# A hybrid attention, mLSTM and Hyena backbone: score, filter-tap and decay products on all 128 rows of the matrix array

## The chip, the cores and the metric

The kernel runs on one core of a Trainium2 chip. The metric is device time in microseconds (us) of one execution, the median of several runs.

## The reference

The program is a two-layer backbone over 512 latent tokens and 256 context tokens of width 1024. What matters here are three small pieces of each layer.

```python
# windowed attention: 8 query heads, 2 key groups, head width 64, blocks of 128 queries
s_loc = einsum('bntkgd,bnskd->bnkgts', qb, kb) * scale      # the block and its neighbours, masked
s_ctx = einsum('bntkgd,bckd->bnkgtc', qb, kc) * scale       # 256 context keys
p = softmax(concatenate([s_sink, s_ctx, s_loc]))
...
# Hyena filter taps: 64 features of every position times w3
h = jnp.sin(freq[1] * (h @ w2 + b2))
h = (h @ w3).reshape(L, HY_ORDER, 2, HY_WIDTH)
...
# mLSTM within a chunk of 128 tokens
dmat = where(tril, b[..., :, None] - b[..., None, :] + ic[..., None, :], -inf)
mt = maximum(a, max(dmat, -1))
s = einsum('bhtd,bhsd->bhts', qc, kc) * exp(dmat - mt[..., None])
```

The rest of a layer is an adaLN-modulated norm, one wide input projection, a gated merge of the three mixers, an output projection and a convolutional FFN.

## The kernel before

Channels lie on the partitions and tokens in the columns. A value that needs full precision is kept as two float32r tiles, a high part and a low part, and a product of two such values is three matrix products: high by high, low by high, high by low. The large products (`kstep`, line 401) run like that with 128 by 128 weights and up to 512 columns; their weights come from memory as 512 KB tiles and are split on ScalarE (line 339) and VectorE (line 340).

The work of the mixers is written as Python generators. Each is a "lane", and `tick` lets lanes emit some of their instructions after each step of the large products, at rates written in `RATE`. So TensorE's queue is one static order in which mixer products are strewn between large products, and an operation that waits holds all that are behind it. Tiles come from pools: `T` tiles are 768 columns wide, `H` tiles 512, with counts by stage in `SIZES`; a new tile waits until one of its kind is free.

Three places use only half of the array's 128 rows.

- **Scores.** Heads are 64 wide, so `stacked` (line 792) lays a query's 64 high rows and 64 low rows over the 128 partitions. A key's high rows stand there twice (two copies by DMA from the POOL queue, lines 801 and 802), so one product on 128 rows gives (q high + q low) by k high (line 1037). The key's low parts stand once, in one tile: group 0 on rows 0 to 63, group 1 on rows 64 to 127. Line 1038 multiplies them with the query's high rows alone, on 64 rows, into the same columns. An item of `att_mix` is a block of 128 queries, a pair of heads and a key group. A latent item has four such pairs of products (two heads, context keys and local keys) and masks added by bfloat16 products (line 1049); a context item has two pairs. Layer 0 has 16 latent and 8 context items, layer 1 has 16 latent ones. The scores go to one PSUM tile with a single buffer, which the maxima (VectorE, line 1063) and exponentials (ScalarE, line 1067) read before the next item's scores may be written. Then come `normalize`, transposes (line 1093), their copies into `H` tiles named pT (lines 1103 and 1105) and the products with the values (line 1119), whose outputs take 64 columns of the array.
- **Filter taps.** `filter_taps` multiplies 64 features with w3. `hd` holds their high rows over their low rows; `w3h` and `w3l` hold the weights' parts, which came twice, on all 128 rows. Line 654 takes all rows of `hd` and `w3h`, line 655 the upper 64 rows of `hd` and `w3l`. There are four sets of 4 products for the 512 tokens in each layer and four sets of 2 for the context in layer 0: 40 in all.
- **Decays.** `ml_gates` leaves the running maxima as two tensors of 64 rows (high and low parts) in memory, and `ml_load` reads them into two tiles of 64 rows from the POOL queue. In `prep`, for each of 4 heads, 2 directions and each group of up to four chunks, two products on 64 rows (line 1351) with a column of a negated identity (`nident`, 64 rows, line 281) spread the row of one head over all partitions, first the high parts and then the low ones, and a bfloat16 product adds the mask (line 1353). Layer 0 has groups of 512 and of 256 columns, layer 1 only groups of 512: 24 groups.

The stages of a layer are: A (gates, with norms, modulation and filters beside them), the attention's projections (`att_proj`, then `att_finish`), the attention beside the mLSTM's projections, the mLSTM beside the Hyena projections, E (Hyena and merges), and the FFN, in which layer 0 also runs layer 1's filters.

Of the kernel before, what the change touches and what calls it, by code (L numbers as in the profile page):

```python
# [32 lines left out]
# order of the m-tiles of the stacked [D_MODEL, 128] weights of a layer  # L33
# [12 lines left out]
# columns of the packed per-channel vectors of a layer  # L46
# [11 lines left out]
# ---------------------------------------------------------------- constants of the shapes  # L58
# [70 lines left out]
# ---------------------------------------------------------------- layout of the inputs  # L129
# [82 lines left out]
# ---------------------------------------------------------------- the program  # L212
class Two:
    """latent and context columns in two tiles"""
# [24 lines left out]
class Prog:  # L239
# [3 lines left out]
    SIZES = {'A0': (18, 26), 'A1': (8, 41), 'mix': (20, 21), 'E': (16, 29), 'ffn0': (20, 23), 'ffn1': (30, 0)}  # L243
# [17 lines left out]
    def __init__(self, tc, es, aps, dbg=None):  # L261
        self.tc, self.nc, self.a, self.dbg = tc, tc.nc, aps, dbg or {}
        nc = self.nc
        self.n = 0
        self.lanes, self.deferred, self.late = [], [], []
        pool = lambda name, bufs, **k: es.enter_context(tc.tile_pool(name=name, bufs=bufs, **k))
        self.cp = pool("const", 1)
        self.wp = pool("weights", 2)
        self.hp = pool("hl", 16)
        self.dp = pool("dram", 1, space=DRAM)  # L270
        self.pg = pool("psg", 3, space=PSUM)
        c = self.cp
        a = aps
        self.cv = c.tile([P, 16], F32, name="cv")
        nc.sync.dma_start(self.cv, a["cv"])
        self.ident = c.tile([P, P], F32, name="ident")
        make_identity(nc, self.ident)
        self.identb = c.tile([P, P], BF16, name="identb")
        nc.vector.tensor_copy(self.identb, self.ident)
        self.nident = c.tile([64, 64], F32R, name="nident")  # L280
        nc.vector.tensor_scalar(self.nident, self.ident[:64, :64], -1.0, None, op0=ALU.mult)
        self.ones = c.tile([P, P], F32, name="ones")
        nc.vector.memset(self.ones, 1.0)
        self.eps = c.tile([P, 1], F32, name="eps")
        nc.vector.memset(self.eps, EPS)
        self.sv = [c.tile([P, NSV], F32, name=f"sv{l}") for l in range(DEPTH)]
        self.fg = c.tile([P, KD], F32, name="fg")
        self.rope = c.tile([P, 2, SEQ], F32, name="rope")
        self.maskb = c.tile([P, 2, P], BF16, name="maskb")
        self.mod = [c.tile([P, 48, 2], F32, name=f"mod{l}") for l in range(DEPTH)]  # L290
        self.A = {(l, i): c.tile([P, KD, 2], F32, name=f"A{l}{i}") for l in range(DEPTH) for i in (1, 2)}
        self.sil = c.tile([P, KD, 32], F32, name="sil")
        self.g_dram = {}
# [8 lines left out]
    # ---- small helpers  # L302
# [39 lines left out]
    # ---- weaving of the mixers' work into the stream of matrix products  # L342
# [26 lines left out]
    def fill(self, n):  # L369
        """work put by for the places where the products have to wait"""  # L370
        for _ in range(n):
            next(self.spare, None)
# [11 lines left out]
    # ---- GEMM  # L384
# [34 lines left out]
    def proj_first(self, l, ms, parts):  # L419
        """three m-tiles, part by part, two of them k outermost: the operands may still be coming"""  # L420
        ws = [self.weight(self.a["wA"][l, m]) for m in ms]
        joint = parts[-1][1] <= 512
        if joint:
            one = [self.G() for _ in ms]
        outs = [[] for _ in ms]
        for i, (lo, hi, _) in enumerate(parts):
            if i:
                self.run_deferred()
            pss = [ps[:, lo:hi] for ps in one] if joint else [self.G() if i == 0 else self.M() for _ in ms]
            for group in ((0, 1), (2,)) if i == 0 else ((0,), (1,), (2,)):  # L430
                for k in range(KD):
                    for j in group:
                        self.kstep(pss[j], ws[j], slice(k * P, k * P + P), self.hlh[k], self.hll[k], lo, hi, k == 0, k == KD - 1)
                    self.tick(3 * len(group) * max(0.109, (hi - lo) * 0.422e-3))
            for o, ps in zip(outs, pss):
                o.append((lo, hi, ps))
        self.run_deferred()
        return [[(0, parts[-1][1], ps)] for ps in one] if joint else outs
# [12 lines left out]
    def fine_parts(self, l):  # L451
        """parts that the end of one product and the start of the next go through one after the other"""
        return self.parts(l) if l < DEPTH - 1 else [(0, 256, 0), (256, SEQ, 0)]

    # ---- adaLN modulation
# [9 lines left out]
    def ada(self, l, blocks):  # L465
        """blocks of 512 of the six vectors; the groups of k-tiles side by side in the array's columns"""
# [25 lines left out]
    # ---- norms  # L492
# [56 lines left out]
    # ---- Hyena filters in the frequency domain  # L549
# [20 lines left out]
    def filters(self, l, L, resident, overlap):  # L570
        """spectra of the filters, by order and half of the channels: filter taps, then their DFT"""
# [17 lines left out]
        # [high; low] parts of the 64 features, which came twice  # L589
# [27 lines left out]
    def filter_taps(self, l, L, hd, dec, it, out):  # L617
# [21 lines left out]
        for t in range(nT + 1):  # L639
# [12 lines left out]
            if t < nT:  # L652
                ps = self.M()
                nc.tensor.matmul(ps, hd[:, t * P:(t + 1) * P], w3h, start=True, stop=False)
                nc.tensor.matmul(ps, hd[0:64, t * P:(t + 1) * P], w3l[0:64], start=False, stop=True)
# [23 lines left out]
    def filter_dft(self, l, L, gc, it, sd):  # L679
# [9 lines left out]
        def dft(c, half):  # L689
            """cos / -sin, high and low parts, [tau tile][k] of a half of the taps"""  # L690
# [40 lines left out]
    # ---- projections  # L731
# [4 lines left out]
    def conv(self, l, dst, outs, w, b):  # L736
        """width-3 depthwise convolution of the tokens, the latent and the context ones apart"""
# [40 lines left out]
    def rope_swap(self, q):  # L778
        """the halves of each head's channels in each other's place"""
# [12 lines left out]
    def stacked(self, x, n, key):  # L792
        """per kv group the parts of 64 channels over all the partitions:
        a query's high part (at its group's place) and its low part; a key's high part twice, and apart its low part"""
        nc = self.nc
        top, bot, low = self.T("x0", dt=F32R), self.T("x1", dt=F32R), self.T("xl", dt=F32R)
        for h, t in ((0, top), (64, bot)):
            nc.scalar.copy(t[h:h + 64, :n], x[h:h + 64, :n])
            nc.vector.tensor_tensor(low[h:h + 64, :n], x[h:h + 64, :n], t[h:h + 64, :n].bitcast(F32), op=ALU.subtract)
        if key:  # L800
            nc.gpsimd.dma_start(top[64:128, :n], top[0:64, :n])
            nc.gpsimd.dma_start(bot[0:64, :n], bot[64:128, :n])
            return top, bot, low
# [7 lines left out]
    def tok_major(self, src, dst):  # L811
        """the six chunks of columns of src, transposed, into a tile [P, 6, P] or into six tiles"""
# [21 lines left out]
    def fold(self, kind, half, base, L):  # L834
        """tiles of a half of the channels (kind 0: v, 1: x1), folded about the centre of the tokens"""
# [12 lines left out]
    def fold_tok(self, fs, H, jt):  # L848
        """one token tile of the folded channels, token-major [sum | difference]"""
# [7 lines left out]
    def pair_products(self, ps, g, sub, parts):  # L857
        """complex products of [real | imaginary] columns, each half split into its parts on its own"""
# [28 lines left out]
    def hy_mix(self, l, out):  # L887
        """the halves of the channels one after the other, the next one's start within the second order of the one before;
        the short sequence's halves side by side"""
# [122 lines left out]
    # ---- attention  # L1012
    def att_mix(self, l, out):
        """software pipeline over (block of queries, pair of heads, kv group)"""
# [11 lines left out]
        def scores(it):  # L1026
            qb, p, kv = it
            ds_ = slice(kv * 64, kv * 64 + 64)
# [3 lines left out]
            # head 0: the local keys end and its context keys begin at 512; head 1: context keys, then local keys from 1024  # L1032
            kh, kl = k[kv], k[2]

            def dots(o, j, ks, n, stop):
                qh = q[2 * p + j][kv]
                nc.tensor.matmul(ps[:, o:o + n], qh[:, self.chunk(qb)], kh[:, ks], start=True, stop=False)
                nc.tensor.matmul(ps[:, o:o + n], qh[ds_, self.chunk(qb)], kl[ds_, ks], start=False, stop=stop)
# [43 lines left out]
        def transposes(it, i0):  # L1082
# [6 lines left out]
            for i in range(n):  # L1089
                for j in range(2):  # L1090
                    # columns of the block in the row of head j
# [69 lines left out]
    # ---- mLSTM  # L1161
# [35 lines left out]
    def rev_copy(self, f, dst, src):  # L1197
        """[64, 768] rows: forward rows as they are, backward rows turned within the latent and the context part"""
# [19 lines left out]
    def ml_gates(self, l):  # L1218
# [3 lines left out]
        # log sigmoid(f) = min(f, 0) - ln(1 + exp(-|f|))  # L1222
# [51 lines left out]
        # natural token order  # L1274
# [33 lines left out]
    def ml_load(self):  # L1308
# [5 lines left out]
        self.ml["mn"] = [self.T("mn", [64, NT], F32R) for _ in range(2)]  # L1314
        for x in range(2):
            nc.gpsimd.dma_start(self.ml["mn"][x], self.mld[0:64, 2 + x, :])
# [4 lines left out]
    def ml_mix(self, l, out):  # L1321
# [9 lines left out]
        def prep(h):  # L1331
# [12 lines left out]
            for d in range(2):  # L1344
                r = d * 32 + h
                dt = self.T("dt", [P, 6, P])
                for i in range(0, nch, 4):
                    w = min(4, nch - i)
                    pt = self.M()
                    for x in range(2):  # L1350
                        nc.tensor.matmul(pt[:, :w * P], self.nident[:, r:r + 1].to_broadcast([64, P]),
                                         mn[x][:, i * P:(i + w) * P], start=(x == 0), stop=False)
# [9 lines left out]
        def chain(h):  # L1362
# [75 lines left out]
            # channel-major  # L1438
# [57 lines left out]
    def merge(self, l, r, branches, gates, y, b, nxt=None):  # L1496
        """y (+)= 2 sigmoid(gate_r) * (branch_r @ w_branch_r); after the last branch half of y, in high and low parts"""
# [47 lines left out]
    def ffn(self, l, x, part_done):  # L1545
# [6 lines left out]
        def down(c, last, ms=range(KD)):  # L1552
# [14 lines left out]
            if last:  # L1567
                # part by part; the weights stay if there is room for them, or come again
# [17 lines left out]
        for c in range(len(bounds) - 1):  # L1586
            for i in range(bounds[c], bounds[c + 1]):
# [16 lines left out]
                # some of the last but one product is left for the wait for the last one's operands  # L1604
# [165 lines left out]
```

## Time and profile before

| | us |
|---|---|
| median of 3 runs | 2808.58 (2805.72 to 2810.65) |
| span of the profiled execution | 2804.0 |
| TensorE busy | 2695.0 (96%) |
| VectorE busy | 1752.1 (62%) |
| ScalarE busy | 1051.3 (37%) |
| GpSimd busy | 282.1 (10%) |

The profiled execution's own time is not listed apart: its span is 4.6 us under the median. In the rows below, PE is TensorE's matmul, PEld its weight load, DVE VectorE, ACT ScalarE, POOL GpSimd and SP SyncE. "128*64 ... 128x256" is a matmul on 128 rows and 64 columns of the array with a 128 by 256 moving operand. A matmul's printed duration reaches from its start to the modelled end of its results, and the next one begins before that; how long it holds the array is read from one start to the next.

### The profile page before, as it was taken

To read this page: it belongs to the slowest core of one execution; us is meant where nothing else is said; L and a number is where in the kernel's file an instruction comes from. 1 tells how busy PE (TensorE), PEld (TensorE's weight loads), DVE (VectorE), ACT (ScalarE), POOL (GpSimd) and SP (SyncE) were. 2 spreads that over 40 slices of the span, in tenths; PEclk is the share of its full clock that TensorE was granted. 3 is DMA by queue.
4 is the path that set the end of the run, shared out by engine and by line. 5 is a ranking of instruction groups with operands and counts; after the bars stand their busy time and mean duration, and the time that the engine had idled before them with its cause. 6 is when DMAs were issued, how large, how long until landed. Compare 5 with 4: busy or idle time off the path is not lost. (4 is left out here: it accounts for less than half of the span.)

```text
span 2804.0 us, 38203 instructions
## 1 busy us (share of the span) xinstructions
PE 2695.0 (96%) x14762; PEld 2199.1 (78%) x14762; DVE 1752.1 (62%) x3076; ACT 1051.3 (37%) x1893; POOL 282.1 (10%) x297
## 2 busy tenths in 40 slices
PE   6899999999999998999999999999999999999998
PEld 2678787778888886787888887777787778888887
DVE  5685554556457765767667566655447477665666
ACT  4344343445323233433233234534345233533333
POOL 3241110000000301011101000210000002000000
PEclk8999999999999999999999999999999999999999
DMA  7555331122436542354443224541222556333332
GB/s 257 168 199 195 108 95 38 38 66 91 151 130 207 174 155 70 116 169 143 132 131 91 68 65 149 185 136 40 76 91 94 185 183 211 98 98 98 97 95 65
DMA packets 153158, 347.66 MB, mean 124 GB/s; under 512 B 15553, under 2 KB 52910, under 8 KB 152976
## 3 DMA queue, kind: packets, MB, share of 16 engines
q1 hardware_dynamic: 132976, 319.03, 34.3%
q0 software_dynamic: 20000, 26.19, 3.7%
q8 instruction: 117, 1.92, 0.3%
q14 instruction: 65, 0.53, 0.1%
HBM read 287.02 MB, written 52.17 MB: 121 GB/s over the span
## 5 line engine op out<-in xcount | busy, mean ns | idle before, releaser
L401 PE MATMUL pg<-hh,wh 128*128 128x512 f32 (+1 forms) x2536 | 923.8, 365 | 7.9 <-ACT hh L339 6.2
L401 PE MATMUL pg<-hlo,wh 128*128 128x512 f32 (+1 forms) x2536 | 900.7, 355 | 4.1 <-DVE hlo L340 3.9
L401 PE MATMUL pg<-hh,wl 128*128 128x512 f32 (+1 forms) x2536 | 898.6, 355 | 0.1
L340 DVE TENSOR_TENSOR wl<-wr,wh 128x1024 fp32r<-128x1024 f32 x294 | 370.3, 1260 | 304.1 <-ACT wh L339 296.2
L401 PEld LDWEIGHTS pg<-hh,wh 128*128 128x128 f32 x2536 | 483.4, 191 | 94.5 <-issue 26.7
L401 PEld LDWEIGHTS pg<-hlo,wh 128*128 128x128 f32 x2536 | 484.3, 191 | 67.2 <-DVE hlo L340 6.8
L401 PEld LDWEIGHTS pg<-hh,wl 128*128 128x128 f32 x2536 | 483.1, 191 | 66.2 <-issue 1.5
L339 ACT CAST wh<-wr 128x1024 fp32r<-128x1024 f32 x294 | 308.8, 1050 | 567.2 <-PE pg L401 525.3
L1527 DVE SCALAR_TENSOR_TENSOR x<-pg,mod,x 128x512 f32<-128x512 f32 (+1 forms) x242 | 149.0, 629 | 113.2 <-PE pg L401 111.0
L401 PE MATMUL pg<-fh,wh 128*128 128x512 f32 (+1 forms) x544 | 194.0, 358 | 8.7 <-DVE x L1527 8.0
L401 PE MATMUL pg<-fl,wh 128*128 128x512 f32 (+1 forms) x544 | 191.6, 352 | 0.0
L401 PE MATMUL pg<-fh,wl 128*128 128x512 f32 (+1 forms) x544 | 190.5, 351 | 0.9 <-DVE wl L340 0.9
L742 ACT ACTIVATE u<-pg,sv 128x512 f32<-128x512 f32 (+1 forms) x165 | 116.6, 708 | 134.9 <-PE pg L401 134.8
L743 DVE SCALAR_TENSOR_TENSOR u<-pg,sv,u 128x511 f32<-128x511 f32 (+1 forms) x165 | 108.3, 658 | 86.2 <-ACT u L742 86.0
L401 PEld LDWEIGHTS pg<-fh,wh 128*128 128x128 f32 x544 | 103.7, 191 | 29.2 <-DVE x L1527 12.1
L1067 ACT ACTIVATE p<-s,sm 128x512 f32<-128x512 f32 (+2 forms) x80 | 55.3, 692 | 171.8 <-DVE sm L1064 142.9
L1063 DVE TENSOR_REDUCE sm<-s 128x1 f32<-128x512 f32 (+2 forms) x80 | 55.2, 690 | 99.5 <-PE s L1049 67.8
L401 PE MATMUL pg<-bh,wh 128*128 128x512 f32 (+1 forms) x320 | 111.7, 381 | 5.6 <-ACT bh L339 3.3
L401 PEld LDWEIGHTS pg<-fh,wl 128*128 128x128 f32 x544 | 103.7, 191 | 15.1 <-DVE wl L340 1.4
L401 PEld LDWEIGHTS pg<-fl,wh 128*128 128x128 f32 x544 | 103.9, 191 | 14.0 <-issue 0.7
L744 DVE SCALAR_TENSOR_TENSOR u<-pg,sv,u 128x511 f32<-128x511 f32 (+1 forms) x165 | 108.7, 660 | 2.5
L401 PE MATMUL pg<-bh,wl 128*128 128x512 f32 (+1 forms) x256 | 94.7, 370 | 0.0
(301 smaller groups left out, 4068.3 us busy)
## 6 DMA issues: line engine op xcount, KB each, us to landing
wr<-in_wA SPq DMA_DIRECT2D x222, 512.0 KB, 3.7
wr<-in_adaw SPq DMA_DIRECT2D x96, 512.0 KB, 4.6
wr<-in_wD SPq DMA_DIRECT2D x48, 512.0 KB, 3.6
wr<-in_wB SPq DMA_DIRECT2D x24, 512.0 KB, 5.2
gates<-gt SPq DMA_DIRECT2D x28, 384.0 KB, 2.7
gc<-in_g POOLq DMA_DIRECT2D x40, 256.0 KB, 3.8
g<-gd SPq DMA_DIRECT2D x40, 256.0 KB, 4.3
g<-gates SPq DMA_DIRECT2D x24, 384.0 KB, 7.7
```

The lines of the kernel that those rows point to most:

```text
L339: nc.scalar.copy(h, src)
L340: (nc.gpsimd if pool else nc.vector).tensor_tensor(l, src, h.bitcast(F32), op=ALU.subtract)
L401: self.nc.tensor.matmul(ps[:, :hi - lo], a[:, ks], b[:, lo:hi], start=(first and i == 0), stop=(last and i == 2))
L742: nc.scalar.activation(dst[:, lo:hi], ps[:, :n], AF.Identity, bias=b, scale=w(1))
L743: V(dst[:, lo + 1:hi], ps[:, 0:n - 1], w(0), dst[:, lo + 1:hi], op0=mul, op1=add)
L744: V(dst[:, lo:hi - 1], ps[:, 1:n], w(2), dst[:, lo:hi - 1], op0=mul, op1=add)
L1063: nc.vector.tensor_reduce(sm[:, j:j + 1], src, axis=AX.X, op=ALU.max)
L1067: nc.scalar.activation(t[:, :w], src, AF.Exp, bias=sm[:, 2 + j:3 + j], scale=0.125, accum_out=sm[:, 4 + j:5 + j])
L1527: self.nc.vector.scalar_tensor_tensor(x[m][:, lo:hi], ps[:, :hi - lo], self.mod[l][:, p * 8 + m, j:j + 1], x[m][:, lo:hi], op0=ALU.mult, o ...
```

## The change

A key's low parts are laid on both halves of the partitions, like its high parts: a second tile "xm" takes group 1, and two more DMAs on the POOL queue copy each tile's 64 rows to its other half. The second score product then takes all 128 rows of the query's tile. The second tap product takes all 128 rows of `hd` and `w3l`. The running maxima's high and low parts are read into the two halves of one tile, the negated identity stands twice, and one product takes the place of two. In the mixers' stage the pool has one more `T` tile and one fewer `H` tile. Comments are dropped.

```diff
-    SIZES = {..., 'mix': (20, 21), ...}
+    SIZES = {..., 'mix': (21, 20), ...}
...
-        self.nident = c.tile([64, 64], F32R, name="nident")
-        nc.vector.tensor_scalar(self.nident, self.ident[:64, :64], -1.0, None, op0=ALU.mult)
+        self.nident = c.tile([P, 64], F32R, name="nident")
+        for h in (0, 64):
+            nc.vector.tensor_scalar(self.nident[h:h + 64, :], self.ident[h:h + 64, h:h + 64], -1.0, None, op0=ALU.mult)
...
-                nc.tensor.matmul(ps, hd[0:64, t * P:(t + 1) * P], w3l[0:64], start=False, stop=True)
+                nc.tensor.matmul(ps, hd[:, t * P:(t + 1) * P], w3l, start=False, stop=True)
...
         top, bot, low = self.T("x0", dt=F32R), self.T("x1", dt=F32R), self.T("xl", dt=F32R)
-        for h, t in ((0, top), (64, bot)):
+        lows = (low, self.T("xm", dt=F32R)) if key else (low, low)
+        for h, t, lw in ((0, top, lows[0]), (64, bot, lows[1])):
             nc.scalar.copy(t[h:h + 64, :n], x[h:h + 64, :n])
-            nc.vector.tensor_tensor(low[h:h + 64, :n], x[h:h + 64, :n], t[h:h + 64, :n].bitcast(F32), op=ALU.subtract)
+            nc.vector.tensor_tensor(lw[h:h + 64, :n], x[h:h + 64, :n], t[h:h + 64, :n].bitcast(F32), op=ALU.subtract)
         if key:
-            nc.gpsimd.dma_start(top[64:128, :n], top[0:64, :n])
-            nc.gpsimd.dma_start(bot[0:64, :n], bot[64:128, :n])
-            return top, bot, low
+            for a, b in ((top, bot), lows):
+                nc.gpsimd.dma_start(a[64:128, :n], a[0:64, :n])
+                nc.gpsimd.dma_start(b[0:64, :n], b[64:128, :n])
+            return (top, bot), lows
...
-            kh, kl = k[kv], k[2]
+            kh, kl = k[0][kv], k[1][kv]
...
-                nc.tensor.matmul(ps[:, o:o + n], qh[ds_, self.chunk(qb)], kl[ds_, ks], start=False, stop=stop)
+                nc.tensor.matmul(ps[:, o:o + n], qh[:, self.chunk(qb)], kl[:, ks], start=False, stop=stop)
...
-        self.ml["mn"] = [self.T("mn", [64, NT], F32R) for _ in range(2)]
+        self.ml["mn"] = self.T("mn", [P, NT], F32R)
         for x in range(2):
-            nc.gpsimd.dma_start(self.ml["mn"][x], self.mld[0:64, 2 + x, :])
+            nc.gpsimd.dma_start(self.ml["mn"][64 * x:64 * x + 64, :], self.mld[0:64, 2 + x, :])
...
-                    for x in range(2):
-                        nc.tensor.matmul(pt[:, :w * P], self.nident[:, r:r + 1].to_broadcast([64, P]),
-                                         mn[x][:, i * P:(i + w) * P], start=(x == 0), stop=False)
+                    nc.tensor.matmul(pt[:, :w * P], self.nident[:, r:r + 1].to_broadcast([P, P]),
+                                     mn[:, i * P:(i + w) * P], start=True, stop=False)
```

## Rows read from the trace of the kernel before

**Rows 1.** The page's first part: busy us, share of the span, instructions.
```profile
PE 2695.0 (96%) x14762; PEld 2199.1 (78%) x14762; DVE 1752.1 (62%) x3076; ACT 1051.3 (37%) x1893; POOL 282.1 (10%) x297
```
**Rows 2.** Busy by stretch: length, PE, PEld, DVE, ACT, POOL, granted clock, DMA share, GB/s.
```profile
381.00:593.00 212.00, 211.89 (x1232) 159.69 (x1230) 109.65 (x269) 81.78 (x236) 4.26 (x7) 1.00 0.17 50
...
1865.00:2029.00 164.00, 162.54 (x908) 119.18 (x906) 87.74 (x190) 65.97 (x169) 7.11 (x16) 0.99 0.22 62
```
**Rows 3.** Timeline of PE, a context item's scores: start, us, engine, line, operation.
```profile
473.20 0.38 PE L1037 MATMUL s<-x,x 128*128 128x256 f32 x1
473.51 0.38 PE L1038 MATMUL s<-xl,x 64*128 64x256 f32 x1
473.82 0.39 PE L1037 MATMUL s<-x,x 128*128 128x256 f32 x1
...
474.45 0.38 PE L401 MATMUL pg<-hh,wh 128*128 128x256 f32 x1
474.67 0.28 PE L401 MATMUL pg<-hlo,wh 128*128 128x256 f32 x1
474.79 0.28 PE L401 MATMUL pg<-hh,wl 128*128 128x256 f32 x1
```
**Rows 4.** Lines 1038 and 655: count, ns min/median/max, first and last start, forms.
```profile
L1038 PE MATMUL s<-xl,x x144: 379/382/442, 381.8 to 2005.8; 64*128 64x256 f32 x112, 64*128 64x384 f32 x32
...
L655 PE MATMUL pm<-w3l,hd x40: 388/498/793, 55.6 to 1472.8; 64*128 64x512 f32 x40
```
**Rows 5.** Timeline of PE, a middle latent item: first score product, first transpose behind it.
```profile
1976.89 0.38 PE L1037 MATMUL s<-x,x 128*128 128x256 f32 x1
...
1979.82 0.60 PE L1093 MATMUL tp<-ident,p 128*128 128x128 f32 x4
```
**Rows 6.** Timeline of PE, one filter tap in the FFN stage.
```profile
1264.02 0.39 PE L654 MATMUL pm<-w3h,hd 128*128 128x512 f32 x1
1264.34 0.49 PE L655 MATMUL pm<-w3l,hd 64*128 64x512 f32 x1
1264.76 0.50 PE L401 MATMUL pg<-hh,wh 128*128 128x512 f32 x1
1265.10 0.40 PE L401 MATMUL pg<-hlo,wh 128*128 128x512 f32 x1
1265.34 0.39 PE L401 MATMUL pg<-hh,wl 128*128 128x512 f32 x1
```
**Rows 7.** Timeline of PE, decays of one direction in layer 0.
```profile
595.73 0.72 PE L1351 MATMUL pm<-mn,nident 64*128 64x512 f32 x2
...
596.70 0.50 PE L1351 MATMUL pm<-mn,nident 64*128 64x256 f32 x2
...
597.35 0.73 PE L1351 MATMUL pm<-mn,nident 64*128 64x512 f32 x2
```
**Rows 8.** Timeline of PE in the first stage, one wait in brackets.
```profile
90.75 1.12 PE L481 MATMUL adaq<-ident,adae 128*128 128x128 f32 x4 [5.97 <-ACT adae L477]
```
**Rows 9.** Waits: us in total, times, longest; 381 to 593 us, then PE in 1865 to 2029.
```profile
DVE sm L1063 <- PE s L1049: 35.9, 16, 4.9
...
PE s L1037 <- DMA x<-xl: 1.4, 1, 1.4
```
**Rows 10.** DMA issues, 1840 to 1872 us: count, KB each, median us to landing.
```profile
x<-x POOLq DMA_DIRECT2D x2, 192.0 KB, 5.4
```
**Rows 11.** Line 281: count, ns min/median/max, first and last start, forms.
```profile
L281 DVE TENSOR_SCALAR nident<-ident x1: 598/598/598, 10.3 to 10.3; 64x64 fp32r<-64x64 f32 x1
```
**Rows 12.** Timelines of DVE, ACT and PE: the softmax of the item of rows 5.
```profile
1980.02 0.82 DVE L1063 TENSOR_REDUCE sm<-s 128x1 f32<-128x640 f32 x1 [3.94 <-PE s L1049]
...
1985.08 0.19 ACT L1067 ACTIVATION_READ_ACCUMULATOR p<-s,sm 128x1 f32 x1
...
1985.32 0.38 PE L1037 MATMUL s<-x,x 128*128 128x256 f32 x1
```
**Rows 13.** Timeline of PEld: the weight load for the product at 474.67 of rows 3.
```profile
474.56 0.19 PEld L401 LDWEIGHTS pg<-hlo,wh 128*128 128x128 f32 x1
```

More of the change, by code (lines that the diff above doesn't have):

```diff
@@ L242 @@
     RATE = ({'filt': 1.587, 'ada': 1.362, 'mlg': 0.55, 'att': 0.92, 'ml': 1.258, 'hy': 0.997}, {'filt': 0.389, 'ada': 0.512, 'mlg': 0.616, 'att': 1.008, 'ml': 2.5, 'hy': 2.149})
-    SIZES = {'A0': (18, 26), 'A1': (8, 41), 'mix': (20, 21), 'E': (16, 29), 'ffn0': (20, 23), 'ffn1': (30, 0)}
+    SIZES = {'A0': (18, 26), 'A1': (8, 41), 'mix': (21, 20), 'E': (16, 29), 'ffn0': (20, 23), 'ffn1': (30, 0)}
     BOUNDS = ((0, 2, 4, 6, 8, 10, 12, 14, 16, 18, 22), (0, 4, 8, 12, 16, 20, 22))
@@ L1027, in scores @@
             qb, p, kv = it
-            ds_ = slice(kv * 64, kv * 64 + 64)
             blocks = blocks_of(qb)
```

## The prediction, made before the kernel ran

> **What bounds the kernel now.** I read the page's busy shares first: TensorE is busy 96% of the span, VectorE 62% and ScalarE 37% [rows 1]. Then I asked for busy time by stretch. In the two attention stages TensorE has work in flight all but 0.1 and 1.5 us, at full clock, with VectorE near half and DMA at 0.17 and 0.22 [rows 2]. So what these stages last is what TensorE's queue takes, and the question is how long each product holds the array. That is in the timeline, from one start to the next. A 256-column product on 128 rows behind another such holds it for 0.12 us (474.67 to 474.79), a 512-column one for some 0.23 (1265.10 to 1265.34 is 0.24). But a score product on 128 rows followed by one on 64 takes 0.31, and one on 64 followed by one on 128 takes 0.31 as well; the first large product behind such a pair still takes 0.22 [rows 3, 6]. Every change of the row count thus costs about 0.2 us, and each half-height product has one on either side. The reader is to see in these rows a stall that no wait is named for: the engine counts as busy through it.
>
> **The change, part by part.**
>
> *Scores.* 144 products go from 64 to 128 rows [rows 4]: four in each of 32 latent items, two in each of 8 context items. A context item's four products reach from 473.20 to 474.45, and the next product adds 0.22: 1.47 us. Afterwards the first still follows a product on 64 columns (that change of shape stays, as does its 0.22), and three and the large one take 0.12: 0.22 + 4 x 0.12 = 0.70. Saved: 0.77 [rows 3]. A middle latent item takes 2.93 us from its first score product to its first transpose [rows 5]. Afterwards: 0.22 + 3 x 0.12 for the context keys, four 384-column products at 0.175 (an estimate midway between 0.12 and 0.23) and four mask products, for which no row shows the price behind a full-height product: 0.05 if they cost what they do now, 0.11 if little less than a 256-column one. That makes 1.48 to 1.72, saved 1.21 to 1.45; I take 1.33, the middle. The 16 items at the edges have two masks and 256 columns, but the same four half-height products, and I give them the same. Sum: 32 x 1.33 + 8 x 0.77 = 48.7 us (45 to 54).
>
> *Taps.* 40 products [rows 4]. High, low and the two large ones behind take 1.32 us; four at 0.23 would take 0.92: 0.40 saved [rows 6]. The first four (from 55.6 us) lie ahead of a wait of 5.97 us for ScalarE [rows 8], which takes up what they give. The other 36 give 14.4 (16 if all count; 6.4 if only the 16 in the FFN stage do, because stage A, with waits of its own, takes the rest).
>
> *Decays.* A direction of layer 0 takes 1.62 us, of which the 512-column group takes 0.97 [rows 7]. With one product for two and no change of rows it is 0.23 + 0.23 + 0.12 + 0.12 = 0.70, saved 0.92; in layer 1, with the 512-column group alone, 0.97 - 0.46 = 0.51. Eight directions each: 7.4 + 4.1 = 11.5 (8 to 12.5; the low end if the mask product still pays a stall on each side).
>
> *What is added.* Two DMAs of 192 KB per layer from the POOL queue, behind the two that are there, which land in 5.4 us in layer 1 [rows 10]. Behind them on POOL stand the rope products and the copies of the queries' low parts. In layer 0 the first scores find all that long landed. In layer 1 TensorE already stands 1.4 us for a query's low copy [rows 9], and whatever is added to that chain it waits longer: 0 if the copies ride beside the rest, up to 5.4 if it stands behind them throughout. I take 1, near the lower end, since they would travel while the queries are still being projected. The second half of `nident` is one more VectorE operation like that of 0.60 us at 10.3 us [rows 11], on an engine that is idle 38% of the span and 580 us before its first reader: nothing, and at most its 0.6. VectorE's subtractions and the DMAs of the maxima stay the same in number; the second tile for the keys is covered by the added T tile, and the maxima need one less.
>
> *Given back.* The saving is taken out of the score block itself. VectorE's first maximum stands waiting for its end now (35.9 us in 16 waits in layer 0) [rows 9], so the softmax starts earlier by as much, and the large products between one block and the next are the same. But the room is small: in the middle item taken above the last exponential ends at 1985.27 and the next item's scores start at 1985.32 [rows 12]. VectorE and ScalarE do the same work in 13% less time, and some weight split will get in the way. I put 3 us for the attention, and 2 for waits of the taps and decays on their evacuations.
>
> *Sum.* 48.7 + 14.4 + 11.5 = 74.6; less 1 + 3 + 2 = 6 leaves 68.6. The profiled span of 2804.0 becomes 2735.4; with the 4.6 us by which the span lies under the median, **2740 us**, 2.4% faster. Its own range: with the upper ends and nothing given back, 54 + 16 + 12.5 = 82.5, that is 2726; with the lower ends (45, 6.4, 8) and 11 given back, 48, that is 2760.
>
> **The rivals.**
>
> *The softmax keeps its own time.* The scores have one PSUM buffer, so a block can't start before the exponentials of the one before have ended. If VectorE and ScalarE are held up by weight splits and copies rather than by the end of the scores, their chain ends where it does now and TensorE waits for it. For: the 0.05 us of room [rows 12]. Against: VectorE is busy for 52% of that stage [rows 2], and its wait names TensorE. If half of each latent block's gain goes so, 32 x 0.66 = 21 in place of the 3: 2758.
>
> *The load no longer overlaps.* Products on the same rows might have to wait for their weights, so that each takes the 0.22 of the product after a change of shape, not 0.12. Then a half-height product gives back 2 x (0.31 - 0.22) = 0.18, 208 of them (144 + 40 + 24) give 37, the 24 dropped products give 16 x 0.23 + 8 x 0.12 = 4.6, and the time is 2767. Against it: in the steady stream all products use the same rows and still start 0.12 apart while each load takes 0.19, and the load at 474.56 starts within the product of 474.45 [rows 3, 13]. The Trainium skill speaks for this rival: "TensorE: Matmul & The Clock Gate", Part 3, "The mechanism", says that a weight load overlaps running matmuls only where the row groups differ. By that rule the time would be the 2767; the rows just named disagree, and they decide.
>
> *The price is not the row count's.* If the 0.31 belonged to something else that stays (the operands' tiles, the same columns of PSUM written twice), only the 24 dropped products would count: 2804, within 0.2%. Against: the large products write the same columns three times in a row at 0.12 [rows 3], and taps and decays, with other tiles, show the same price [rows 6, 7].
>
> *Slower: the missing H tile.* The mixers' stage has 20 H tiles in place of 21. Twelve are held by the mLSTM's keys and values, two items' transposed probabilities take six and the output copies two: 20, with none to spare. If a copy waits until a pair's values are done, a pair is late by up to one item's time, 212 / 24 = 8.8 us [rows 2]: 20 pairs, 176 us, 2916. It outweighs the gain from 3.4 us a pair on. Against: the six are free again before the next pair's first copy, which stands behind the values in TensorE's queue.
>
> **How the numbers follow.** The forecast has 0.76, the softmax 0.13, the load 0.04, the price elsewhere 0.03, the missing tile 0.04, of which I give 0.01 to a stall that just cancels the gain. The range of 2725 to 2762 holds the forecast with its bounds and the softmax rival. A measurement of this kernel can tell some 0.2% (5.6 us) from no change. Faster 0.93, within 0.2% 0.04, slower 0.03.
>
> **What would show it.** Right: score products all on 128 rows and 0.12 us apart at 256 columns, latent blocks of about 1.6 us, the first attention stage about 27 us shorter and the second about 21, 24 decay products in place of 48. Wrong in size: TensorE waiting on the exponentials at its score line (softmax), 0.22 between score products (load), a longer wait for the query's copy in layer 1, or pT copies that wait for TensorE's values (missing tile). The prediction falls if the products on full rows still start 0.31 apart.

## The result, and the profile after

The changed kernel takes 2741.6 us (median of 4 runs, 2739.82 to 2744.43) against 2807.82 for the kernel before in the same runs: a ratio of 0.9766, 95% interval 0.9753 to 0.978, 66 us. The prediction was 2740 (2725 to 2762). The profiled span went from 2804.0 to 2738.1 us.

The page's first part (busy us, share of the span, instructions) and the busy time by stretch (length, PE, PEld, DVE, ACT, POOL, clock, DMA share, GB/s) of the two attention stages of the changed kernel, from the first score to the last value product. They answer to [rows 1, 2]:

```profile
PE 2619.3 (96%) x14738; PEld 2178.8 (80%) x14738; DVE 1750.4 (64%) x3077; ACT 1050.5 (38%) x1893; POOL 284.7 (10%) x301
...
378.50:562.90 184.40, 184.26 (x1229) 151.82 (x1227) 110.01 (x268) 81.28 (x236) 3.95 (x6) 1.00 0.19 57
1821.70:1963.50 141.80, 139.22 (x906) 111.69 (x904) 85.80 (x190) 65.66 (x168) 7.98 (x16) 1.00 0.25 71
```

TensorE is still the bound at 96%; its busy time fell by 75.7 us while it issues only 24 products fewer. VectorE and ScalarE have the same work in stages that are 13% shorter.

The timeline of PE (start, us, engine, line, operation), a context item's scores, which answers to [rows 3]; line 1040 is the product with the high parts, 1041 that with the low parts:

```profile
458.41 0.38 PE L1040 MATMUL s<-x,x 128*128 128x256 f32 x1
458.63 0.28 PE L1041 MATMUL s<-xl,x 128*128 128x256 f32 x1
458.75 0.28 PE L1040 MATMUL s<-x,x 128*128 128x256 f32 x1
458.86 0.28 PE L1041 MATMUL s<-xl,x 128*128 128x256 f32 x1
458.99 0.28 PE L403 MATMUL pg<-hh,wh 128*128 128x256 f32 x1
```

The first product still pays for the value products on 64 columns ahead of it (0.22), and all others start 0.12 apart. A tap in the FFN stage, which answers to [rows 6], and the decays of one direction in layer 0, which answer to [rows 7]:

```profile
1225.03 0.39 PE L656 MATMUL pm<-w3h,hd 128*128 128x512 f32 x1
1225.26 0.40 PE L657 MATMUL pm<-w3l,hd 128*128 128x512 f32 x1
1225.49 0.39 PE L403 MATMUL pg<-hh,wh 128*128 128x512 f32 x1
1225.72 0.39 PE L403 MATMUL pg<-hlo,wh 128*128 128x512 f32 x1
```

```profile
565.57 0.48 PE L1353 MATMUL pm<-mn,nident 128*128 128x512 f32 x1
...
565.93 0.47 PE L1353 MATMUL pm<-mn,nident 128*128 128x256 f32 x1
...
566.28 0.48 PE L1353 MATMUL pm<-mn,nident 128*128 128x512 f32 x1
```

The direction takes 566.28 - 565.57 = 0.71 us where it took 1.62; the forecast was 0.70.

Where the 66 us went is read from stretches between the starts of the same instructions in both traces. A score product here is any product into the score tile, masks included; an evacuation is the copy of a finished sum out of TensorE's accumulator (PSUM), here ScalarE's part of it:

| stretch | before, us | after, us | saved | forecast |
|---|---|---|---|---|
| first to last score product, layer 0 | 203.5 | 176.8 | 26.7 | 27.4 |
| the same, layer 1 | 140.9 | 119.3 | 21.7 | 21.3 |
| fifth to last tap, stage A | 210.9 | 207.7 | 3.2 | 8.0 |
| first to last tap, layer 1's filters | 312.4 | 307.5 | 4.9 | 6.4 |
| last value product to the last Hyena evacuation, layer 0 | 146.7 | 140.7 | 6.0 | 7.4 |
| the same, layer 1 | 148.3 | 146.8 | 1.5 | 4.1 |

The forecast column is gross, ahead of the 6 us given back. The rows sum to 64.0; the 1.9 us that are left of 65.9 lie in stretches that the change doesn't touch. The one that differs most reaches from the last Hyena evacuation of layer 0 to layer 1's first tap: 419.2 us at a mean granted clock of TensorE of 0.96 before, 416.4 at 0.97 after. Only the edit to the modulation products below reaches into it; in the other twelve profiled executions it takes from 415.1 us (clock 0.98) to 421.6 (0.95). So a few us of any difference here go with the clock that an execution was granted.

### The profile page after: what moved, and what is told of

Read it like the earlier page. It is cut to its first block, busy times and chain, and to the rows that moved or that the text cites. A ratio compares the mean times of both kernels' runs of the same rounds, so it can differ in the third digit from the quotient of the medians.

```text
span 2738.1 us, 38162 instructions
## 1 busy us (share of the span) xinstructions
PE 2619.3 (96%) x14738; PEld 2178.8 (80%) x14738; DVE 1750.4 (64%) x3077; ACT 1050.5 (38%) x1893; POOL 284.7 (10%) x301
```

## The experiments

**The scores alone** (the kernel before with the edits to `SIZES`, `stacked` and `scores` of the diff above).

> The kernel before with the change of the scores alone (keys' low parts doubled, one more T and one fewer H tile). If each half-height product costs two changes of the row count and the softmax keeps up, 48.7 us less the 4 given back: about 2763, with the two attention stages 27 and 21 us shorter. If the softmax kept its own time, about 2781. If the price belonged to the operands' tiles, 2808.

Measured: 2757.47 us, ratio 0.9829 (0.9816 to 0.9842), 49 us. The two score stretches are 26.7 and 19.7 us shorter; of the rest, the largest part is the 2.8 us by which the stretch named above came out shorter here too. So the scores give what the price by row changes says, and the softmax does not keep its own time.

**The taps alone.**

```diff
-                nc.tensor.matmul(ps, hd[0:64, t * P:(t + 1) * P], w3l[0:64], start=False, stop=True)
+                nc.tensor.matmul(ps, hd[:, t * P:(t + 1) * P], w3l, start=False, stop=True)
```

> The kernel before with the change of the tap products alone. By the step of the prediction 14.4 us less some waits: about 2795. By the trace of the changed kernel, in which stage A is only 3 us shorter and the stretch of layer 1's taps 5 to 7, about 2799, with TensorE waiting longer in stage A for the taps' sums and weights.

Measured: 2797.83 us, ratio 0.9968 (0.9953 to 0.9983), 9 us. The interval (5 to 13 us) leaves out the forecast's 14.4, but holds both expected times; the runs spread from 2786.81 to 2805.04. The trace decides: the tap stretches are 3.1 us shorter in stage A and 4.9 in layer 1's filters (the changed kernel: 3.2 and 4.9), which falls on the second expectation.

**The decays alone** (the edits to `nident`, `ml_load` and `prep`).

> The kernel before with the change of the decays alone. By the step of the prediction 11.5 us: about 2797. By the trace of the changed kernel, 6 in layer 0 and next to nothing in layer 1, where the end of the mLSTM stage waits for VectorE: about 2802.

Measured: 2795.55 us, ratio 0.9966 (0.9954 to 0.9979), 11 us. The median alone would speak for the forecast, but the interval (6 to 13 us) holds both values. The trace decides: the mLSTM stages are 5.8 and 1.5 us shorter, as in the changed kernel, and the rest of the 11 lies in stretches that the decays don't touch.

**Only the row count undone**: doubled keys, their DMAs and the pools as changed.

```diff
+            ds_ = slice(kv * 64, kv * 64 + 64)
...
-                nc.tensor.matmul(ps[:, o:o + n], qh[:, self.chunk(qb)], kl[:, ks], start=False, stop=stop)
+                nc.tensor.matmul(ps[:, o:o + n], qh[ds_, self.chunk(qb)], kl[ds_, ks], start=False, stop=stop)
```

> The changed kernel, but the second score product takes only the 64 rows of its group again; the doubled key tiles, their DMAs and the pool sizes stay as changed. If the price is that of the row count, all of the scores' gain goes: 2742 + 48 = 2790, with 0.31 us from a score product to the next at 256 columns. If it lay in the tiles, their layout or the pool sizes, 2742.

Measured: 2789.17 us, ratio 0.9939 (0.9926 to 0.9952): 47.6 us above the changed kernel. The timeline of PE has the old spacing back, now with the tile "xm":

```profile
387.70 0.39 PE L1041 MATMUL s<-x,x 128*128 128x256 f32 x1
388.02 0.38 PE L1042 MATMUL s<-xm,x 64*128 64x256 f32 x1
388.33 0.38 PE L1041 MATMUL s<-x,x 128*128 128x256 f32 x1
388.65 0.38 PE L1042 MATMUL s<-xm,x 64*128 64x256 f32 x1
```

Nothing differs from the changed kernel but the rows that a product takes, so the gain of the scores is the row count's, and the doubling as such costs or gives nothing that these runs could tell.

**Fewer changes, same half-height products**: the kernel before with a latent item's products in another order.

```diff
-            for j in range(2):
-                dots(512 + j * 256, j, slice(SEQ, NT), CTX, True)
...
+                for low in (False, True):
+                    dots(512, 0, slice(SEQ, NT), CTX, True, (low,))
+                    for j, o in ((0, 512 - nloc * P), (1, 1024)):
+                        dots(o, j, slice(b0 * P, b1 * P + P), nloc * P, False, (low,))
...
+                dots(768, 1, slice(SEQ, NT), CTX, True)
```

> The kernel before with its 64-row products kept, but a latent item's products in another order: three products on 128 rows, then their three on 64 rows, then the masks, then the fourth pair. 144 half-height products stay; the changes of the row count fall from eight to four in each of the 32 latent items. If the price is per change, 4 x 0.2 x 32 = 25 us go: about 2783. If each half-height product costs its price wherever it stands, 2808.

Measured: 2785.85 us, ratio 0.9924 (0.991 to 0.9937), 23 us; the score stretches are 12.1 and 12.6 us shorter, 24.7 together. The timeline of PE:

```profile
386.00 0.51 PE L1038 MATMUL s<-x,x 128*128 128x256 f32 x3
386.44 0.62 PE L1040 MATMUL s<-xl,x 64*128 64x256 f32 x3
386.99 0.28 PE L1055 MATMUL s<-maskb,identb 128*128 128x128 bf16 x2
387.09 0.36 PE L1038 MATMUL s<-x,x 128*128 128x256 f32 x1
387.38 0.38 PE L1040 MATMUL s<-xl,x 64*128 64x256 f32 x1
387.69 0.50 PE L401 MATMUL pg<-hh,wh 128*128 128x512 f32 x1
```

The last of the three products on 64 rows starts at 386.78:

```profile
386.78 0.28 PE L1040 MATMUL s<-xl,x 64*128 64x256 f32 x1
```

Three products on 128 rows take 0.44 and three on 64 take 0.55; one of each, in the last pair, takes 0.29 + 0.31 = 0.60. Within the three on 64 rows, the first takes 0.22, the second 0.12 and the last, ahead of the next change, 0.21. The price is paid per change of the row count and not per half-height product: half of the gain of the scores was to be had by order alone, with no copy. It divides into some 0.1 us ahead of a change and 0.1 behind it.

**The other change of shape: value products on all columns.** They take 64 columns of the array for each group, which leaves a stall on either side. Here the values stand in one tile as group 0, zeros, group 1, so that each group's product can fill 128 columns.

```diff
-                    ds_ = slice(g * 64, g * 64 + 64)
-                    nc.tensor.matmul(po[ds_, 0:256], v[:, b, ds_], s2[g]["pT", i], start=(i == 0), stop=(i == len(blocks) - 1))
+                    nc.tensor.matmul(po[:, 0:256], v[:, b, 64 * g:64 * g + 128], s2[g]["pT", i], start=(i == 0 and g == 0),
+                                     stop=(i == len(blocks) - 1 and g == 1))
```

> The changed kernel, with the values laid so that a product with them fills all 128 columns (the other group's 64 columns are zeros), and 20 T and 19 H tiles to make room. If a change of the column count costs like one of rows, 20 groups of value products lose a stall on each side, 0.2 to 0.4 each less 0.015 for each product that ran beside another: about 2737. If one H tile fewer makes copies wait for a pair's values, slower than 2742.

Measured: 2774.16 us, ratio 0.988 (0.9867 to 0.9894): 32.6 us slower than the changed kernel. The timeline of PE, first the value products of one pair of items in the changed kernel (16, up to the score product at 458.41 shown above), then in this one (20, up to the score product behind them):

```profile
456.53 1.95 PE L1122 MATMUL po<-pT,vt 128*64 128x256 f32 x16
```

```profile
442.04 4.48 PE L1126 MATMUL po<-pT,vz 128*128 128x256 f32 x20
446.17 0.47 PE L1045 MATMUL s<-x,x 128*128 128x256 f32 x1
```

The expectation was wrong by its price for one product. On half the columns the two groups' products run side by side: their starts lie 7 and 209 ns apart in turn. On all columns they start 215 ns apart, one after the other. There are 320 of them (160 calls in the code, of which the trace records two products each), so 320 x (0.215 - 0.108) = 34 us are lost. The two attention stages, from the first score to the last value product, are 12.5 and 13.8 us longer, 26 together. The other 8 would be the stalls that went, 0.4 us for each of 20 groups, which is the price that was expected of them; it was far outweighed. Of the 6 us between 26 and the measured 33, 5.2 lie in the stretch that the result names as going with the granted clock (421.6 us here). Here half the array was not wasted.

**Modulation products in one go** (each takes 32 columns of the array).

```diff
-                yield 6.0
+            yield 12.0
```

> The changed kernel, with the two groups of modulation products of a block (each on 32 columns of the array) issued together rather than apart. If the changes of shape cost as with the rows, half of 48 groups save 0.4 us each, some 9: about 2733. If TensorE then waits for the weights of the second group, that is given back: 2742 or slower.

Measured: 2764.38 us, ratio 0.9847 (0.9833 to 0.986): 23 us slower than the changed kernel. From the start to stage A's last tap it loses 11 us, with TensorE waiting 16.8 us for ScalarE's copy of the modulation sums (9.4 in the changed kernel), and 9 more by layer 1's attention projections. The scores' stretches are as in the changed kernel. Waits cover whatever the changes of shape gave, so their price isn't to be read here: inconclusive.

**One H tile fewer** (19 in place of 20).

> The changed kernel with 19 H tiles in the mixers' stage in place of 20, all else equal. The rival of the missing tile says that 20 are all in use: with one fewer, copies wait for a pair's values and up to 8.8 us per pair are lost, with TensorE waiting at its transposes. If tiles come free before the next pair needs them, 2742.

Measured: 2744.14 us, ratio 0.9773 (0.976 to 0.9786), no different from the changed kernel; the score stretches are 26.7 and 22.2 us shorter than before, as there. The rival of the missing tile falls: with 19 nothing is lost, so TensorE was not waiting for the one that went.

**The two places where the forecast was not reached.** The waits of PE in stage A of the changed kernel (us in total, times, longest), and in layer 1's mLSTM stage:

```profile
PE pm L656 <- ACT w3h L341: 4.3, 3, 2.7
PE pm L663 <- POOL ab L652: 3.8, 5, 1.7
```

```profile
PE pg L403 <- DVE u L746: 2.2, 2, 1.5
```

The product at line 663 adds up the taps' magnitudes, which GpSimd accumulates; in the kernel before it waits 1.0 us in stage A. The wait for "u", VectorE's part of the Hyena projections' evacuation, isn't there before. Each was taken away by itself, the first by adding on VectorE in layer 0, the second by emitting the mLSTM's steps more thinly in layer 1:

```diff
-                    nc.gpsimd.tensor_tensor(acc, acc, ab, op=ALU.add)
+                    (nc.gpsimd if l else nc.vector).tensor_tensor(acc, acc, ab, op=ALU.add)
```

> The changed kernel with layer 0's sums of the taps' magnitudes added on VectorE (0.7 us each by its other operations of that size) and not on GpSimd (1.3 to 2.0 us). In stage A TensorE waits 3.8 us for these sums, 1.0 before the change, and the taps gave 3.2 us there where 8 were forecast. If that wait is where it went, stage A is 2 to 4 us shorter: 2738. If another wait of the filters' chain stands behind it (their weights' split on ScalarE, 4.3 us), stage A stays as it is.

Measured: 2736.39 us, ratio 0.9748 (0.9732 to 0.9763). The fifth to the last tap of stage A takes 202.4 us, 5.3 less than in the changed kernel, and the wait for GpSimd is gone:

```profile
PE pm L656 <- ACT w3h L341: 5.1, 2, 4.6
PE pp L712 <- ACT sdh L341: 3.2, 4, 1.0
```

That is more than the 4.8 by which the taps had missed their forecast there, and it also took out the 1.0 us of this wait that stood before the change. In the changed kernel one of these waits, of 1.7 us, takes back half of the 3.0 us that the taps had gained up to there.

```diff
-    RATE = (..., {..., 'ml': 2.5, ...})
+    RATE = (..., {..., 'ml': 2.1, ...})
```

> The changed kernel with the mLSTM's lane in layer 1 emitted more thinly (rate 2.1 in place of 2.5). In that stage TensorE now waits 2.2 us for VectorE's evacuations of the Hyena projections, which it does not before the change; the decays gave 1.5 us there where 4.1 were forecast. If these waits come from VectorE being crowded by the mLSTM's steps, they go and the stage is some 2 us shorter: 2740. If they are the evacuations' own, or if the lane then runs over the end of the stage, no gain or a loss.

Measured: 2737.32 us, ratio 0.9751 (0.9733 to 0.9768). The stretch to the last Hyena evacuation takes 145.4 us, 1.4 less; the waits for "u" are gone, and the one left has grown from 4.1 us in three to

```profile
PE pm L1446 <- DVE hs L1437: 5.1, 4, 1.3
```

This fits a crowded VectorE, and half of what the decays missed comes back. By their times alone neither this run nor the one before is told from the changed kernel, since the intervals overlap; the stretches tell. That the rest is held by the mLSTM's own chain is what this row says, but it wasn't tried apart.

**Both edits.**

> Both of the two edits before on the changed kernel: 2 us in layer 1's mLSTM stage and 2 to 4 in stage A, 2736, if neither is given back later; 2742 if both are.

Measured: 2734.46 us (2728.75 to 2740.43), ratio 0.9737 (0.9717 to 0.9757): the fastest here, with stage A's stretch at 202.5 and the mLSTM's at 145.4 us. Its interval and the changed kernel's overlap too, so that the 7 us between the medians rest on the two stretches (5.2 and 1.4 us) more than on the times.

## Why the prediction was right

*The price.* The step that carried the sum, that each change of the row count costs some 0.2 us and nothing else in the products changes, holds by each test: row count undone with all else kept, 47.6 of the scores' 48.4 us return; half of the changes taken out by order, half of the gain comes. Middle latent blocks now take 1.45 to 1.59 us where 1.48 to 1.72 were forecast. The price of a mask behind a full-height product lies between the two bounds: in the block at 1901.12, two masks take 0.09 from the first start to the next product, as before, but that product then takes 0.26 where others of its 384 columns take 0.18.

*The rivals.* The load still overlaps: full-height score products start 0.12 apart, where the rival wanted 0.22 and 2767 us. The Trainium skill, "TensorE: Matmul & The Clock Gate", Part 3, "The mechanism", has a weight load overlap running products only where the row groups differ; the rows of before and of after disagree with it. The rival of a price that lies elsewhere fell with the row count undone, that of the missing tile with 19 tiles. The softmax took almost nothing: the waits of PE in layer 1's attention are

```profile
PE s L1040 <- DMA x<-xl: 1.6, 1, 1.6
PE s L1040 <- ACT p L1070: 0.9, 1, 0.9
```

and in layer 0's there are none on the engine itself. The 3 us put down for it, and the 1 for the two more DMAs (1.6 us of waiting in place of 1.4 [rows 9]; they landed in 6.2 and 6.9 us, under way ahead of the query's copies), were hardly needed.

*The mis-sized terms.* Scores: 48.7 less 4 forecast, 48.4 measured. Taps: 14.4 forecast, 8.1 measured. Decays: 11.5 forecast, 7.5 measured. Of the taps and decays together 10.3 us were given back, where the prediction put 2. The page has TensorE idle for 118.8 us of its span where it was 109.0, which is as much. The price of a tap (1.32 to 0.92 us) and of a direction (1.62 to 0.71) was right where TensorE was the bound. What failed is the line "2 for waits of the taps and decays on their evacuations", which was put down with no row behind it: in stage A the next in line was GpSimd's sum of magnitudes, in layer 1's mLSTM stage VectorE's evacuations, as the last runs showed. Of the 1.5 us missing from layer 1's taps, the trace shows more than half: the first three taps are 0.8 us ahead, and just behind them a wait for VectorE that was not there before takes it all back:

```profile
1126.54 0.50 PE L403 MATMUL pg<-fh,wh 128*128 128x512 f32 x1 [0.60 <-DVE x L1529]
```

So 2740 against 2741.6 owes a part to two errors that cancel: about 4 us too much taken off for the attention, about 8 too little for the taps and decays, and 2 from stretches that the change doesn't touch. That leaves the span 2.7 us over the forecast; the median stands 3.5 us over the span where 4.6 were added, and the rest is 1.6. The mechanism was right; that the number came so near is in part luck.

## What to carry to other kernels

Read how long a matrix product holds the array from one start to the next, not from its duration or its engine's busy share: a stall at a change of the array's shape had no wait to its name here and counted as busy. Where half-height products stand singly between full ones, give them all rows, or put them next to each other; but look first whether two halves run side by side, since then filling the array makes it slower. Price what is given back stage by stage, by the engine that is next in each, and not with one small figure for all.

## What the runs showed of the hardware that was not expected

Two products on different halves of the columns run at the same time (starts 7 ns apart, then 209), and the same products on all columns take 215 ns each. Those have float32 operands; the float32r score products of the same 256 columns start 0.12 us apart on the full array. So a product of two float32 operands, which the trace records as two, holds the full array for 0.43 us. Half-height products in a row cost no more than full ones, except at the ends of the row: of three, the first took 0.22 us, the second 0.12 and the last 0.21.
